# One more seven-product pair in the first half of each four-group feed-forward part

## The chip, the cores and the metric

The kernel runs on one core of one Trainium2 chip. A time is the device time of one execution in microseconds (us). A profiled execution also has a span, from its first to its last instruction.

## What is computed

A two-layer causal decoder trunk on 256 tokens of width 2048, all in float32. Layer 0 mixes by gated spatial products and memory attention, layer 1 by latent attention and memory attention. Each layer ends with the gated feed-forward block that the change touches:

```python
def conv_ffn(h, w_up, cw, cb, w_down):      # h (256, 2048), D_FF = 5632
    a = h @ w_up                            # (256, 11264): gate and value halves
    ap = jnp.pad(a, ((0, 0), (CONV_W - 1, 0), (0, 0)))
    c = sum(ap[:, k:k + S] * cw[k] for k in range(CONV_W)) + cb
    gate, val = c[..., :D_FF], c[..., D_FF:]
    return (jax.nn.silu(gate) * val) @ w_down
...
x = x + conv_ffn(rmsnorm(x, g_ffn[l]), w_ffn_up[l], conv_w[l], conv_b[l], w_ffn_down[l])
```

## The kernel before

**Precision.** A float32 product is made of three TensorE products. An operand is split into a high part (ScalarE, ACT below, copies it to the `fp32r` type) and a low part (VectorE, DVE below, subtracts the high part from the operand), and high x high, high x low and low x high are added in PSUM. Weights come through `raw` (the float32 block that SP's queue loads, 4 buffers, in the down product also `gate`, 2 buffers) and are split to `whi` (4 buffers) and `wlo` (5 buffers).

**Parts.** The 5632 inner columns of the feed-forward block are worked off in parts of 4, 4 and 3 groups of 512 (`FF_GROUPS`). For each part the kernel makes the up product (per group one run of 8 chunks for the gate and one for the value, a chunk being 512 KB of weights and 24 matmuls of 256 columns), then `ev` makes the gated result `h`, and then `down_phase` runs twice: the first half for output columns 0 to 1023, the second half for 1024 to 2047. So there are four four-group parts in the program, two in each layer, in which a half works off 8 pairs of 128-row blocks.

**Pairs.** A plain pair takes 8 block products, 24 matmuls of 512 columns. A seven-product pair (`fast_pair`, a scheme in the manner of Strassen) takes 7, 21 matmuls, but wants sums and differences of its operands. On the side of `h`, `ev` writes quarters of the gated result into the tile `src` (one buffer), makes sums and differences in it, and splits it into a high and a low form of 896 or 1024 columns. On the weight side four sums of half blocks, `t13` and `t24`, are split beside the second row block (`y`) and the left half of the first (`x`). The two parts of this left half go to `one`, which in a four-group part is the same single buffer as `src`. So `one` can only be written after the last read of the `src` before it.

**Where the sums are made.** For three pairs of a first half (`FF_EARLY`) DVE adds them during the part's last up product and they wait in SBUF: two pairs in the tile `sums`, the third in `xs` (2 buffers). For some (`FF_STORED`) they are made during an earlier up product, or during the layer's `w_out` product, and written to DRAM by GpSimd's (POOL's) queue; the half reads them back into `xs` or into `staged` (`FF_STAGED`). A stored case has its loads at chunk n, its four adds at n + 5 and its two stores at n + 8. For the rest (`late_sums`) DVE adds them in the half itself.

**Order.** `FF_FAST` gives for each half the pairs that take seven products, and the order of all of them. Within the engines a list scheduler sets the order of instructions when the program is built; on the chip each engine's queue runs in that order. PSUM has 8 banks: in a half with seven-product pairs four hold the outputs (`e00`, `e01`, `e10`, `e11`) and four hold products that `between` copies to `staged` after the last seven-product pair. `e11` takes plain pairs' products alone. Each output bank is added to the tile `xt` by DVE at the end (`added`).

**The end.** In the last half of layer 1, `Last.evict` makes the squares for the final norm column by column; the last bank comes in two pieces of 256 columns.

Of the kernel before, what the change touches and what calls it, by code (L numbers as in the profile page):

```python
# [8 lines left out]
F32 = mybir.dt.float32  # L9
# [4 lines left out]
ALU = mybir.AluOpType  # L14
AX = mybir.AxisListType

P = 128
D = 2048
# [12 lines left out]
THETA = 10000.0  # L31
EPS = 1e-6
FF_GROUPS = (4, 4, 3)
FF_EARLY = {4: (2, 6, 5), 3: (1, 2, 4)}
FF_STORED = {
# [4 lines left out]
}  # L40
FF_STAGED = {4: (5, 1), 3: (5, 0)}
FF_FAST = {
    4: (((2, 3, 4, 6, 5), (0, 1, 5, 2, 7, 3, 6, 4)), ((2, 3, 4, 6, 5), (0, 2, 1, 3, 5, 4, 7, 6))),
    3: (((1, 2, 4, 5), (0, 3, 1, 2, 4, 5)), ((), (0, 1, 2, 3, 4, 5))),
}

# [35 lines left out]
class Kernel:  # L82
# [119 lines left out]


    def gemm_tm(self, src, nkb, ncol, lhs, evict, nk=2, gain=None, hooks={}, late=0):
        accs = [self.psum() for _ in range(2)]
        nch = nkb // nk
# [56 lines left out]
    def rstd(self, out, sums, n, pool, tag):  # L263
        nc = self.nc
        shape = list(out.shape)
        v = self.tmp(pool, shape, tag + "v", 1)
        r = self.tmp(pool, shape, tag + "r", 1)
        q = self.tmp(pool, shape, tag + "q", 1)
        nc.vector.tensor_scalar(v, sums, 1.0 / n, EPS, ALU.mult, ALU.add)
        nc.scalar.activation(r, v, AF.Sqrt)  # L270
        nc.vector.reciprocal(r, r)
        nc.vector.tensor_tensor(q, r, r, ALU.mult)
        nc.vector.scalar_tensor_tensor(q, q, -0.5, v, ALU.mult, ALU.mult)
        nc.vector.scalar_tensor_tensor(out, q, 1.5, r, ALU.add, ALU.mult)
# [487 lines left out]
    def stored_sums(self, l, case, pool):  # L762
        part, k, ph = case
        dn = self.t["w_ffn_down"][l][sum(FF_GROUPS[:part]) * 512 :]
        order = mybir.DependencyInfo(mybir.DependencyClass.NoSync, mybir.DependencyReason.DATA)
        add = lambda o, a, b: self.tc.keep_in_program_order(self.nc.vector.tensor_tensor(o, a, b, ALU.add))  # L766
        left, right, c = slice(0, 512), slice(512, 1024), 1024 * ph
        held = []

        def load(out, in_):  # L770
            ins = self.nc.sync.dma_start(out=out, in_=in_)
            self.tc.add_manual_dep(ins.ins, self.last_raw, order, reason="behind")

        def loads():
            held.extend(self.tmp(pool(), [P, 1024], "xs", 2) for _ in range(2))
            t13, t24 = held
            x, y = (dn[(2 * k + i) * P : (2 * k + i + 1) * P, c : c + 1024] for i in range(2))
            load(out=t13, in_=x)
            load(out=t24[:, left], in_=y[:, right])
            load(out=t24[:, right], in_=y[:, left])  # L780

        def adds():
            t13, t24 = held
            add(t13[:, left], t13[:, left], t13[:, right])
            add(t13[:, right], t13[:, right], t24[:, left])
            add(t24[:, left], t24[:, left], t13[:, left])
            add(t24[:, right], t24[:, right], t24[:, left])

        def stores():
            kept = self.stored[l, *case] = self.dram.tile([P, 2, 1024], F32, name=self.uid("stored"))  # L790
            for i in range(2):
                self.nc.gpsimd.dma_start(out=kept[:, i], in_=held[i])  # L792

        return loads, adds, stores

    def storing(self, l, part, pool):
        hooks = {}
        for n, case in FF_STORED[part].items():
            loads, adds, stores = self.stored_sums(l, case, pool)
            for m, f in (n, loads), (n + 5, adds), (n + 8, stores):  # L800
                hooks.setdefault(m // 8, {}).setdefault(m % 8, []).append(f)
        return hooks

    def late_sums(self, raws, pool):
# [29 lines left out]
    def down_phase(self, dn, col, order, fast, lhs, rhs, pool, fp, between, evict, finish, late=0, late_gains=None, hooks={}, sums={}, stored={}):  # L834
# [3 lines left out]
        left, right = slice(0, 512), slice(512, 1024)  # L838
# [4 lines left out]
        total = dict(todo)  # L843
# [15 lines left out]
        kept = []  # L859
        last_fast = [k for k in order if k in fast][-1:]  # L860
        for n, k in enumerate(order):
# [8 lines left out]
            load = lambda o, a: self.behind(self.nc.sync.dma_start(out=o, in_=a))  # L870
            row = lambda i, c: load(raws[i][:, :c], dn[(2 * k + i) * P : (2 * k + i + 1) * P, col : col + c])
            blocks = sums.get(k)
            if kept_sums is None:
                row(0, 1024 if blocks is None else 512)
                row(1, 1024)
            else:
                if (k, col // 1024) == FF_STAGED[len(order) // 2]:
                    tile = self.tokens.staged[:, 1].rearrange("p m c -> p (m c)")
                    blocks = [tile[:, i * 1024 : (i + 1) * 1024] for i in range(2)]
                else:  # L880
                    blocks = [self.tmp(pool, [P, 1024], "xs", 2) for _ in range(2)]
                row(1, 1024)
                for i in (1, 0):
                    load(blocks[i], kept_sums[:, i])
                row(0, 512)
# [26 lines left out]
        with self.tc.manual_schedule(engines={ET.PE, ET.DVE, ET.Activation}):  # L912
# [9 lines left out]
            k, ws = kept[-1]  # L922
# [510 lines left out]


class Tokens:
    places = ("hx0", 0), ("hx1", 0), ("hx2", 0), ("hx3", 0)

    def __init__(self, kernel, pool):
        self.k, self.nc, self.pool = kernel, kernel.nc, pool
# [134 lines left out]


class Last(Tokens):
    places = ("kT1", 32), ("mv1", 0), ("hx", 0), ("hx3", 0)

    def __init__(self, kernel, pool):
        super().__init__(kernel, pool)  # L1580
# [19 lines left out]
    def evict(self, tb, half, acc, piece=None, meanwhile=lambda: None):  # L1600
        k, nc, xt, sums = self.k, self.nc, self.xt, self.sums
        c0, n = (0, 512) if piece is None else (256 * piece, 256)
        j, o = self.added(tb, half, acc, c0, n)
        c = slice(j * 512 + c0, j * 512 + c0 + n)
        if not self.last:
            return
        one = lambda x: x[:, tb : tb + 1]
        part, r, q, v, gb = self.part, self.r, self.q, self.v, self.gb
        junk = k.tmp(self.pool, [P, 512], "fjunk", 2)
        if piece == 1:  # L1610
            nc.vector.tensor_tensor_reduce(
                out=junk[:, :n], in0=o, in1=o, scale=-0.5 / D, scalar=one(part), op0=ALU.mult, op1=ALU.add, accum_out=one(v)
            )
        else:
            nc.scalar.activation(junk[:, :n], o, AF.Square, accum_out=sums[:, tb, j : j + 1])
        if piece == 0:
            self.added(tb, half, acc, 256, 256)
        meanwhile()
        if j < 3 and not (tb and j == 2):
            nc.vector.tensor_tensor(o, o, gb[:, c], ALU.mult)  # L1620
# [4 lines left out]
            if tb:  # L1625
                nc.vector.tensor_tensor(o, o, gb[:, c], ALU.mult)
        if j == 3:
            if piece != 1:
                total = one(part) if piece == 0 else one(v)
                nc.vector.tensor_scalar(total, sums[:, tb, 3:4], -0.5 / D, one(part), ALU.mult, ALU.add)  # L1630
            if piece == 0:
                return
            nc.scalar.activation(one(r), one(v), AF.Sqrt, scale=-2.0)
            nc.vector.reciprocal(one(r), one(r))
            nc.vector.scalar_tensor_tensor(one(q), one(r), one(r), one(v), ALU.mult, ALU.mult)
            nc.vector.scalar_tensor_tensor(one(r), one(q), 1.5, one(r), ALU.add, ALU.mult)
# [36 lines left out]
```

## Time and profile before

| | |
|---|---|
| median of 3 runs | 2021.81 us (2021.78 to 2022.23) |
| profiled execution, its own time | 2022.45 us |
| its span | 2020.7 us |
| TensorE (PE) busy | 2010.5 us, 99% of the span |
| DVE busy | 1665.6 us, 82% |
| ACT busy | 1184.9 us, 59% |
| POOL busy | 129.1 us, 6% |
| moved by DMA | 463.27 MB, 229 GB/s over the span |

PE, PEld (its weight loads), DVE, ACT, POOL and SP are the engines of the profile; SP only issues transfers. A line such as L719 is a line of the kernel, and often a helper's: all splits of weights in the down product have L718 (ACT) and L719 (DVE). Matmuls are pipelined, so the duration of one is longer than the distance from its start to the start of the next. In a view in order of time a row gives start, duration, engine, line, operation, output and inputs.

### The profile page before, as it was taken

Reading aid. Unit: us, or ns where it says so; the run is one execution under the profiler, and the core shown is the slowest. Engines: PE = TensorE matmul, PEld = TensorE weight load, DVE = VectorE, ACT = ScalarE, POOL = GpSimd, SP = SyncE. Lnnn points to the kernel's source line nnn. Section 1 sums busy time; section 2 is a strip of 40 time slices with the busy share of each in tenths; the row PEclk is TensorE's granted clock in tenths of the full one; section 3 lists DMA queues with packets and bytes.
Section 4 is the critical chain, followed back from the end, with each engine's and each line's share of the span. In section 5 each row is a group of like instructions: output and inputs, shape, how many; then the busy total and the mean of one; then the engine's idle time right before and its main releaser. Section 6 shows DMA issues by size and latency. Waiting matters only on the chain.

```text
span 2020.7 us, 38415 instructions
## 1 busy us (share of the span) xinstructions
PE 2010.5 (99%) x15098; PEld 1905.3 (94%) x15098; DVE 1665.6 (82%) x2519; ACT 1184.9 (59%) x1687; POOL 129.1 (6%) x205
## 2 busy tenths in 40 slices
PE   9999999999999999999999999999999999999998
PEld 8989999999989999899989999999988999889996
DVE  6866767788898788988988787778889878898897
ACT  6754744555665556655576675455566555665565
POOL 0000013100000000000002142400000000000000
PEclk9999999999999999999999999999999999999999
DMA  8775567888668786678566636788867878667865
GB/s 256 232 217 180 166 217 254 232 293 276 210 235 266 246 275 211 233 234 261 185 224 187 183 113 203 235 242 288 275 206 237 273 237 275 206 235 233 275 187 179
DMA packets 269897, 463.27 MB, mean 229 GB/s; under 512 B 77774, under 2 KB 85268, under 8 KB 269716
## 3 DMA queue, kind: packets, MB, share of 16 engines
q1 hardware_dynamic: 264340, 441.40, 68.6%
q0 software_dynamic: 5184, 18.88, 2.6%
q8 instruction: 118, 1.93, 0.4%
q14 instruction: 63, 0.52, 0.1%
q10 hardware_dynamic: 192, 0.54, 0.1%
HBM read 435.06 MB, written 20.97 MB: 226 GB/s over the span
## 4 chain that ended last, share of the span: by engine, by line
PE 98%; DVE 1%; ACT 1%; DMA 0%; issue 0%; SPq 0%; ACTq 0%; DVEq 0%
PE ps L166 22%; PE ps L167 22%; PE ps L169 22%; PE ps L850 7%; PE ps L851 7%; PE ps L852 7%; PE ps L198 2%; PE ps L199 2%; PE ps L200 2%; PE ps L533 1%; DMA raw<-in_w_ffn_down 0%; PE ps L613 0%; PE ps L612 0%; PE ps L611 0%; PE ps L415 0%; PE ps L1324 0%
## 5 line engine op out<-in xcount | busy, mean ns | idle before, releaser
L127 ACT ACTIVATE whi<-raw 128x1024 fp32r<-128x1024 f32 x484 | 513.7, 1062 | 528.7 <-PE ps L167 387.3
L128 DVE TENSOR_TENSOR wlo<-raw,whi 128x1024 fp32r<-128x1024 f32 x484 | 597.1, 1238 | 204.2 <-ACT whi L127 200.6
L166 PE MATMUL ps<-xhl,whi 128*128 128x256 f32 x3264 | 763.3, 277 | 0.0
L167 PE MATMUL ps<-xhl,whi 128*128 128x256 f32 x3264 | 761.6, 276 | 0.0
L167 PEld LDWEIGHTS ps<-xhl,whi 128*128 128x128 f32 x3264 | 612.8, 188 | 0.4
L166 PEld LDWEIGHTS ps<-xhl,whi 128*128 128x128 f32 x3264 | 612.8, 188 | 0.4
L169 PE MATMUL ps<-xhl,wlo 128*128 128x256 f32 x3264 | 438.0, 276 | 0.0
L169 PEld LDWEIGHTS ps<-xhl,wlo 128*128 128x128 f32 x3264 | 401.1, 188 | 0.0
L851 PE MATMUL ps<-wlo,h 128*128 128x512 f32 x354 | 137.1, 388 | 0.1
L719 DVE TENSOR_TENSOR wlo<-raw,whi 128x1024 fp32r<-128x1024 f32 x94 | 113.9, 1219 | 20.9 <-ACT whi L718 20.0
L718 ACT ACTIVATE whi<-raw 128x1024 fp32r<-128x1024 f32 x94 | 98.4, 1054 | 52.7 <-PE ps L167 32.2
L166 PE MATMUL ps<-mainhl,whi 128*128 128x256 f32 x512 | 119.7, 277 | 0.0
L167 PE MATMUL ps<-mainhl,whi 128*128 128x256 f32 x512 | 119.3, 276 | 0.0
L852 PE MATMUL ps<-whi,h 128*128 128x512 f32 (+1 forms) x306 | 118.4, 388 | 0.0
L967 ACT ACTIVATE c<-a,cT 128x256 f32<-128x256 f32 x176 | 99.0, 591 | 29.4 <-DVE a L246 28.4
L850 PE MATMUL ps<-whi,h 128*128 128x512 f32 x354 | 108.3, 389 | 0.0
L167 PEld LDWEIGHTS ps<-mainhl,whi 128*128 128x128 f32 x512 | 96.0, 188 | 0.0
L166 PEld LDWEIGHTS ps<-mainhl,whi 128*128 128x128 f32 x512 | 95.9, 188 | 0.0
L792 POOL DMA_DIRECT2D stored<-xs x36 | 19.8, 550 | 1158.9 <-DVE xs L766 985.1
L718 ACT ACTIVATE whi<-xs 128x1024 fp32r<-128x1024 f32 x60 | 62.7, 1058 | 47.6 <-DVE xs L808 23.7
L133 DVE SCALAR_TENSOR_TENSOR wlo<-raw,gT,whi 128x512 fp32r<-128x512 f32 x96 | 71.0, 779 | 21.3 <-ACT whi L132 21.2
L852 PE MATMUL ps<-whi,hhx 128*128 128x512 f32 x216 | 84.0, 389 | 0.0
(401 smaller groups left out, 3131.6 us busy)
## 6 DMA issues: line engine op xcount, KB each, us to landing
raw<-in_w_ffn_up SPq DMA_DIRECT2D x352, 512.0 KB, 4.6
raw<-in_w_ffn_down SPq DMA_DIRECT2D x102, 512.0 KB, 5.8
raw<-in_w_out SPq DMA_DIRECT2D x64, 512.0 KB, 4.4
raw<-in_w_in_a SPq DMA_DIRECT2D x56, 512.0 KB, 4.4
gate<-in_w_ffn_down SPq DMA_DIRECT2D x38, 512.0 KB, 5.0
stored<-xs POOLq DMA_DIRECT2D x36, 512.0 KB, 5.3
raw<-in_w_mem_kv SPq DMA_DIRECT2D x31, 512.0 KB, 3.6
xs<-in_w_ffn_down SPq DMA_DIRECT2D x24, 512.0 KB, 6.5
```

Source lines behind the costliest of these rows:

```text
L127: nc.scalar.activation(hi[:, :n], raw[:, :n], AF.Copy)
L128: nc.vector.tensor_tensor(lo[:, :n], raw[:, :n], hi[:, :n].bitcast(F32), ALU.subtract)
L133: nc.vector.scalar_tensor_tensor(lo[:, s], raw[:, s], gains[k], hi[:, s].bitcast(F32), ALU.mult, ALU.subtract)
L166: mm(acc[:, :S], wh, x[:, :S], start=first, stop=False)
L167: mm(acc[:, :S], wh, x[:, S:], start=False, stop=False)
L169: mm(acc[:, :S], wl, x[:, :S], start=False, stop=last)
L718: self.behind(self.nc.scalar.activation(hi, w, AF.Copy))
L719: self.behind(self.nc.vector.tensor_tensor(lo, w, hi.bitcast(F32), ALU.subtract))
L850: mm(o, xh, wh, start=start, stop=False)
L851: mm(o, xh, wl, start=False, stop=False)
L852: mm(o, xl, wh, start=False, stop=stop)
L967: nc.scalar.activation(c, a, AF.Identity, scale=w(2), bias=w(3))
```

## The change

In the first half of the four-group parts pair 7 becomes a seven-product pair, so 6 of 8 are. The order becomes: the plain pairs 0 and 1 first, then 2, 5, 4, 3, 6, 7. The early pairs are 2, 5 and 4 instead of 2, 6 and 5. The pairs 3, 6 and 7 read stored sums, 3 and 7 into the two halves of `staged`, 6 into `xs`; before, only pair 3 did, and pair 4 had late sums. The second halves stay as they were. So 12 cases a layer are stored for the four-group parts instead of 8, spaced by 8 chunks instead of 11 to 14, and a case's loads and stores are put into the program one by one (n, n + 1, n + 5, n + 6, n + 7). The forms of `h` for pair 7 take 2 x 1024 columns, so a fifth tile `hx4` (`hx2` in layer 1) is used; to make room for it, two temporaries of `rstd` take the ring `sq`. In `Last.evict` the term of the first piece is added after DVE has taken in the second piece.

```diff
-FF_EARLY = {4: (2, 6, 5), 3: (1, 2, 4)}
+FF_EARLY = {4: (2, 5, 4), 3: (1, 2, 4)}
...
-    1: {8: (1, 2, 1), 22: (1, 5, 1), 36: (1, 4, 1)},
+    1: {2: (1, 6, 0), 10: (1, 7, 0), 18: (1, 2, 1), 26: (1, 5, 1), 34: (1, 4, 1)},
...
-FF_STAGED = {4: (5, 1), 3: (5, 0)}
+FF_STAGED = {4: {(3, 0): 1, (7, 0): 0, (5, 1): 1}, 3: {(5, 0): 1}}
...
-    4: (((2, 3, 4, 6, 5), (0, 1, 5, 2, 7, 3, 6, 4)), ((2, 3, 4, 6, 5), (0, 2, 1, 3, 5, 4, 7, 6))),
+    4: (((2, 3, 4, 6, 5, 7), (0, 1, 2, 5, 4, 3, 6, 7)), ((2, 3, 4, 6, 5), (0, 2, 1, 3, 5, 4, 7, 6))),
...
-        v = self.tmp(pool, shape, tag + "v", 1)
+        v, q = (self.tmp(pool, shape, *(("sq", 2) if tag == "rb" else (tag + x, 1))) for x in "vq")
         r = self.tmp(pool, shape, tag + "r", 1)
-        q = self.tmp(pool, shape, tag + "q", 1)
...
-            loads, adds, stores = self.stored_sums(l, case, pool)
-            for m, f in (n, loads), (n + 5, adds), (n + 8, stores):
-                hooks.setdefault(m // 8, {}).setdefault(m % 8, []).append(f)
+            for m, f in zip((0, 1, 5, 6, 7), self.stored_sums(l, case, pool)):
+                hooks.setdefault((n + m) // 8, {}).setdefault((n + m) % 8, []).append(f)
...
-                if (k, col // 1024) == FF_STAGED[len(order) // 2]:
-                    tile = self.tokens.staged[:, 1].rearrange("p m c -> p (m c)")
+                home = FF_STAGED[len(order) // 2].get((k, col // 1024))
+                if home is not None:
+                    tile = self.tokens.staged[:, home].rearrange("p m c -> p (m c)")
...
-    places = ("hx0", 0), ("hx1", 0), ("hx2", 0), ("hx3", 0)
+    places = ("hx0", 0), ("hx1", 0), ("hx2", 0), ("hx3", 0), ("hx4", 0)
...
         if piece == 1:
+            nc.vector.tensor_scalar(one(part), sums[:, tb, 3:4], -0.5 / D, one(part), ALU.mult, ALU.add)
             nc.vector.tensor_tensor_reduce(
...
         if piece == 0:
             self.added(tb, half, acc, 256, 256)
+            return
...
-            if piece != 1:
-                total = one(part) if piece == 0 else one(v)
-                nc.vector.tensor_scalar(total, sums[:, tb, 3:4], -0.5 / D, one(part), ALU.mult, ALU.add)
-            if piece == 0:
-                return
+            if piece is None:
+                nc.vector.tensor_scalar(one(v), sums[:, tb, 3:4], -0.5 / D, one(part), ALU.mult, ALU.add)
```

Three places show how the instructions move; all four four-group parts have them in the same order, and the first is shown. DVE, at the start of the first half, before. `src_6516` is the quarter tile of pair 6, the pair whose `h` is made last in seven-product form; `wlo_6634`, `wlo_6638` and `wlo_6642` are the low parts of `y`, `t24` and `t13` of pair 5, the half's first seven-product pair; `src_6645` is the low part of its left half of `x`; `hhx_584` is the plain `h` of pair 7:

```order
L719 TENSOR_TENSOR wlo_6634<-raw_6630,whi_6633 128x1024
L989 TENSOR_TENSOR gate_5969<-gate_5969,c_6532 128x256
L989 TENSOR_TENSOR gate_5969<-gate_5969,c_6541 128x256
L719 TENSOR_TENSOR wlo_6638<-xs_6292,whi_6637 128x1024
L1008 TENSOR_TENSOR h_4226<-src_6516,h_4226 128x896
L255 TENSOR_TENSOR hhx_584_4230<-gate_5969,hhx_584_4230 128x256 x2
L719 TENSOR_TENSOR wlo_6642<-xs_6291,whi_6641 128x1024
L719 TENSOR_TENSOR src_6645<-raw_6629,src_6645 128x512
```

The same place of the changed kernel. `src_6542` is pair 6's quarter tile and `src_6562` pair 7's, `ps_6580` is the bank `e11`, and `src_6673` is the left half of `x` of pair 2, now the first seven-product pair:

```order
L718 TENSOR_TENSOR wlo_6662<-raw_6658,whi_6661 128x1024
L718 TENSOR_TENSOR wlo_6666<-sums_6030,whi_6665 128x1024
L1008 TENSOR_TENSOR h_4239<-src_6542,h_4239 128x896
L996 TENSOR_TENSOR src_6562<-gate_5995,c_6558 128x2x128
L1000 TENSOR_TENSOR src_6562<-gate_5995,c_6566 128x256
L1503 TENSOR_TENSOR xt<-ps_6580,xt 128x512
L718 TENSOR_TENSOR wlo_6670<-sums_6030,whi_6669 128x1024
L1002 TENSOR_TENSOR src_6562<-src_6562 128x256
L1003 TENSOR_TENSOR src_6562<-src_6562 128x128
L1004 TENSOR_TENSOR src_6562<-src_6562 128x128
L1008 TENSOR_TENSOR hhx_587_4242<-src_6562,hhx_586_4241 128x1024
L718 TENSOR_TENSOR src_6673<-raw_6657,src_6673 128x512
```

Between pair 6's low part and the first `x` stand now seven rows of pair 7's quarters and the bank `e11`, beside `t13`. ACT has its own side of it in the changed kernel: the high part of pair 7's `h` (out of `src_6562`), then the high part of `x` into the same buffer, then `y` and `t24` of the next pair, pair 5:

```order
L1007 ACTIVATE h_4239<-src_6542 128x896
L717 ACTIVATE whi_6669<-sums_6030 128x1024
L1007 ACTIVATE hhx_586_4241<-src_6562 128x1024
L717 ACTIVATE src_6673<-raw_6657 128x512
L717 ACTIVATE whi_6701<-raw_6698 128x1024
L717 ACTIVATE whi_6705<-sums_6030 128x1024
```

Behind the copy of `x` stand the splits that pair 5 needs first. PE, the last rows of pair 2 and the first of pair 5 in the changed kernel (`whi_6669` is the high part of `t13`, `ps_6581` the bank of the product with `x`):

```order
L849 MATMUL ps_6582<-whi_6669,h_4239 128x512
L849 MATMUL ps_6584<-whi_6669,h_4239 128x512
L850 MATMUL ps_6582<-wlo_6670,h_4239 128x512
L851 MATMUL ps_6582<-whi_6669,h_4239 128x512
L850 MATMUL ps_6584<-wlo_6670,h_4239 128x512
L851 MATMUL ps_6584<-whi_6669,h_4239 128x512
L849 MATMUL ps_6581<-src_6673,h_4239 128x512
L850 MATMUL ps_6581<-src_6673,h_4239 128x512
L851 MATMUL ps_6581<-src_6673,h_4239 128x512
L849 MATMUL ps_6577<-whi_6701,h_4239 128x512
```

The three products with `x` are the 19th to 21st of the pair; the second of them reads the low part. Before, counted from the start of the first seven-product pair, they were the 15th, 22nd and 23rd, with first matmuls of the next pair between them. The transfers of the half's second part on SP's queue, changed kernel, from the loads of pair 4 (`gate`) to those of pair 7:

```order
L869 DMA gate_6737<-in_w_ffn_down 128x512
L869 DMA gate_6738<-in_w_ffn_down 128x1024
L869 DMA raw_6778<-in_w_ffn_down 128x1024
L869 DMA staged_6576<-stored_5057 128x1024 x2
L869 DMA raw_6777<-in_w_ffn_down 128x512
L869 DMA raw_6820<-in_w_ffn_down 128x1024
L869 DMA xs_6822<-stored_5341 128x1024
L869 DMA xs_6821<-stored_5341 128x1024
L869 DMA raw_6819<-in_w_ffn_down 128x512
L869 DMA gate_6864<-in_w_ffn_down 128x1024
L869 DMA staged_6576<-stored_5638 128x1024 x2
L869 DMA gate_6863<-in_w_ffn_down 128x512
```

Three pairs in a row read 512 KB + 1 MB + 256 KB each; `staged` takes the memory of the early tile `sums` of pairs 2 and 5, and `xs` that of pair 4.

More of the change, by code (lines that the diff above doesn't have):

```diff
@@ L772, in load, with loads @@
             self.tc.add_manual_dep(ins.ins, self.last_raw, order, reason="behind")
[L774 to L780, printed above, removed]
+        def loads(i):
+            held.append(self.tmp(pool(), [P, 1024], "xs", 2))
+            w = dn[(2 * k + i) * P : (2 * k + i + 1) * P, c : c + 1024]
+            if i == 0:
+                load(out=held[0], in_=w)
+            else:
+                load(out=held[1][:, left], in_=w[:, right])
+                load(out=held[1][:, right], in_=w[:, left])
         def adds():
@@ L787, in adds, with stores @@
             add(t24[:, right], t24[:, right], t24[:, left])
[L789 to L794, printed above, removed]
+        def stores(i):
+            if i == 0:
+                self.stored[l, *case] = self.dram.tile([P, 2, 1024], F32, name=self.uid("stored"))
+            self.nc.gpsimd.dma_start(out=self.stored[l, *case][:, i], in_=held[i])
+        return [lambda: loads(0), lambda: loads(1), adds, lambda: stores(0), lambda: stores(1)]
     def storing(self, l, part, pool):
@@ L1576 @@
 class Last(Tokens):
-    places = ("kT1", 32), ("mv1", 0), ("hx", 0), ("hx3", 0)
+    places = ("kT1", 32), ("mv1", 0), ("hx", 0), ("hx2", 0), ("hx3", 0)
     def __init__(self, kernel, pool):
```

4 rows, old and new, of the table FF_STORED are left out of this document.

## The prediction

> **What bounds the kernel now.** I read the page first (parts 1 and 5), then the list of who waited for whom, then a table of stretches, then the first four-group part in order of time.
>
> ```profile
> span 2020.7 us, 38415 instructions
> PE 2010.5 (99%) x15098; PEld 1905.3 (94%) x15098; DVE 1665.6 (82%) x2519; ACT 1184.9 (59%) x1687; POOL 129.1 (6%) x205
> ...
> L851 PE MATMUL ps<-wlo,h 128*128 128x512 f32 x354 | 137.1, 388 | 0.1
> ```
>
> The profiled execution took 2022.45 us, 1.75 over its span and 0.64 over the median of 2021.81. TensorE is busy nearly throughout, and the list of its waits is short:
>
> ```profile
> PE ps L500 <- DVE ones L297: 1.1, 1, 1.1
> PE ps L850 <- ACT staged L1482: 0.2, 1, 0.2
> PE ps L613 <- DVE pT L255: 0.2, 1, 0.2
> ```
>
> So a matmul that goes is a gain, and any wait of PE is a full loss: no slack later takes it up. Up product, first half, second half of the first four-group part, and two stretches of the next up product (us, busy time by engine, clock, DMA share, GB/s):
>
> ```profile
> core 0: us, PE busy (x) PEld busy (x) DVE busy (x) ACT busy (x) POOL busy (x), PEclk, DMA share, GB/s
> 354.00:528.00 174.00, 174.00 (x1536) 173.95 (x1535) 146.10 (x221) 95.77 (x123) 9.60 (x14) 1.00 0.83 259
> 528.10:568.30 40.20, 40.20 (x179) 32.99 (x178) 36.51 (x52) 26.97 (x34) 0.00 (x0) 1.00 0.56 190
> 568.30:608.50 40.20, 40.20 (x179) 33.15 (x178) 36.87 (x40) 26.69 (x31) 0.00 (x0) 1.00 0.78 268
> ...
> 608.70:630.45 21.75, 21.75 (x193) 21.73 (x192) 21.17 (x24) 10.73 (x13) 0.00 (x0) 1.00 0.84 281
> ...
> 717.45:739.20 21.75, 21.75 (x195) 21.75 (x194) 15.26 (x24) 11.99 (x17) 0.53 (x1) 1.00 0.97 331
> ```
>
> In the halves DVE is busy 91% of the time, so it cannot run far ahead.
>
> **The matmuls removed.** 3 per first half, 12 in all; the program has 12 fewer. Their price is not the mean of 388 ns, which overlaps the next matmul, but the distance of starts:
>
> ```profile
> 528.11 0.40 PE L850 MATMUL ps<-whi,hhx 128*128 128x512 f32 x1
> ...
> 538.78 0.39 PE L852 MATMUL ps<-whi,hhx 128*128 128x512 f32 x1
> 539.01 0.39 PE L850 MATMUL ps<-whi,h 128*128 128x512 f32 x1
> ...
> 542.18 0.39 PE L850 MATMUL ps<-src,h 128*128 128x512 f32 x1
> ...
> 568.28 0.39 PE L850 MATMUL ps<-whi,hhx 128*128 128x512 f32 x1
> ```
>
> The first row opens the first half, the last the second: 40.17 us for 3 x 24 + 5 x 21 = 177 matmuls, 0.227 each. So 12 x 0.227 = 2.72 us are saved. The Trainium skill (TensorE: Matmul & The Clock Gate, "Wait — 56ns, not 53.3ns?") gives 215.7 ns from start to start at 512 columns and a warm clock; with it the term would be 2.59. The trace's 227 decides.
>
> **The new wait.** The third and fourth rows above are the last matmul of plain pair 1 and the first of the first seven-product pair, the fifth its first product with the left half of `x`. What feeds it (first rows DVE, last two ACT):
>
> ```profile
> 534.92 1.22 DVE L719 TENSOR_TENSOR wlo<-raw,whi 128x1024 fp32r<-128x1024 f32 x1
> ...
> 536.73 1.21 DVE L719 TENSOR_TENSOR wlo<-xs,whi 128x1024 fp32r<-128x1024 f32 x1
> 537.86 1.08 DVE L1008 TENSOR_TENSOR h<-src,h 128x896 fp32r<-128x896 f32 x1
> ...
> 539.62 1.23 DVE L719 TENSOR_TENSOR wlo<-xs,whi 128x1024 fp32r<-128x1024 f32 x1
> 540.77 0.69 DVE L719 TENSOR_TENSOR src<-raw,src 128x512 fp32r<-128x512 f32 x1
> ```
>
> ```profile
> 538.53 1.06 ACT L718 ACTIVATE whi<-xs 128x1024 fp32r<-128x1024 f32 x1 [1.27 <-PE ps L852]
> 539.50 0.62 ACT L718 ACTIVATE src<-raw 128x512 fp32r<-128x512 f32 x1
> ```
>
> Now `x` is copied into `src` at 539.50, after pair 6's low part has left it (538.94), and is ready at 540.12, 2 us before its matmul at 542.18. In the changed program pair 7's quarters go through the same buffer in between. Their durations, and that of an output bank's addition:
>
> ```profile
> L1002 DVE TENSOR_TENSOR src<-src x28: 407/416/420, 448.2 to 1961.2; 128x256 f32<-128x256 f32 x28
> L1003 DVE TENSOR_TENSOR src<-src x28: 272/283/292, 449.3 to 1963.2; 128x128 f32<-128x128 f32 x28
> ...
> L1007 ACT ACTIVATE h<-src x28: 934/940/1046, 452.2 to 1966.3; 128x896 fp32r<-128x896 f32 x20, 128x1024 fp32r<-128x1024 f32 x8
> L1008 DVE TENSOR_TENSOR h<-src,h x24: 1079/1084/1219, 453.5 to 1967.7; 128x896 fp32r<-128x896 f32 x16, 128x1024 fp32r<-128x1024 f32 x8
> ```
>
> ```profile
> 554.97 0.68 DVE L1503 TENSOR_TENSOR xt<-ps,xt 128x512 f32<-128x512 f32 x1
> ```
>
> DVE, in the new order and in the old one's time: `y` at 534.92 as before, `t24` 1.13 later (the distance between the rows 536.73 and 537.86), pair 6's low part 537.18 to 538.26, two quarter rows of 0.42 to 539.0. Then `e11`, which waits for pair 1's last matmul (538.78 + 0.39 = 539.17): to 539.9. `t13` to 541.0. Three quarter rows, each reading what the one ahead wrote, 0.42 + 0.28 + 0.28: to 542.0. ACT's high part of 1024 columns, 1.05: to 543.07. DVE's low part, 1.22: to 544.33. Only now is the buffer free: ACT copies `x` (0.62) to 544.98, DVE subtracts (0.69) to 545.70.
>
> PE wants the high part at 539.01 + 18 x 0.227 = 543.09 and gets it at 545.02: 1.93. The low part, one matmul later, at 545.74 instead of 545.25: 0.49. Behind the copy of `x` ACT has the splits of the next pair: `y` is there in time, `t24` at 546.91 and not 546.65 (ACT's splits come 0.97 apart, as 538.53 and 539.50 do): 0.3. Together 2.7 us in a part, and the order is the same in all four: +10.9. If the three quarter rows overlap and `e11` costs nothing it is 1.8 (total 7.2); if each handover on the chain costs 0.1 more, 3.6 (14.4). I take 2.7, by the rows of the same operations.
>
> **Smaller terms.** With pair 4's late sums a small stall goes:
>
> ```profile
> 562.93 2.01 ACT L718 ACTIVATE whi<-xs 128x1024 fp32r<-128x1024 f32 x2 [2.42 <-DVE xs L808]
> ...
> 563.49 1.29 PE L850 MATMUL ps<-whi,h 128*128 128x512 f32 x4
> ```
>
> Four such matmuls take 3 x 0.227 + 0.39 = 1.07, so it is 0.2 in a part, 0.85 in four (bounds 0 and 1.2). At the end DVE no longer stands before the last piece:
>
> ```profile
> 2013.12 0.21 DVE L1630 TENSOR_SCALAR fpart<-fsums,fpart 128x1 f32<-128x1 f32 x1 [0.30 <-ACT fjunk L1615]
> 2013.25 0.41 DVE L1503 TENSOR_TENSOR xt<-ps,xt 128x256 f32<-128x256 f32 x1
> 2013.69 0.48 DVE L1611 CUSTOM_DVE_ANT_0 fjunk<-xt,fpart 128x256 f32<-128x256 f32 x1
> ```
>
> The piece can be added from about 2012.75 on, the small row follows at 2013.15, and the last one comes at 2013.42: -0.25 (bounds -0.4 and +0.1).
>
> The four more stored cases a layer cost DVE four adds of 0.68 each, ACT nothing, and SP's queue waits for a store before the next case's loads. I cost them at nothing, because the splits of the up product run ahead until the buffers are full:
>
> ```profile
> ACT whi L127 <- PE ps L167: 387.3, 283, 3.3
> ACT whi L127 <- DMA raw<-in_w_ffn_up: 62.8, 40, 6.4
> ```
>
> A wait of 6.4 us for a load passes without a row of PE. If the cover goes: one stretch, 608.70, has DVE at 21.17 of 21.75; with 2.7 more it overruns by 2.1, twice in the program, 4.2 at most. The changed temporaries of `rstd`, the fifth tile and `w_out`'s third case add no instruction that PE waits for (0 to 0.5).
>
> Sum: -2.72 + 10.9 - 0.85 - 0.25 = +7.1. Own time 2022.45 + 7.1 = 2029.5; against the median 2028.9.
>
> **Rivals.**
> *The chain is covered* (0.11). The scheduler may rightly count on `x` in time, and handovers may overlap more than I assume. Break-even is a stall of (2.72 + 0.85 + 0.25) / 4 = 0.95 us a part, so `x` would have to come 1.8 us earlier. Against it: each step waits for the one ahead through one buffer, and the chain's ACT and DVE rows are measured. Without any stall: 2021.81 - 3.8 = 2018.0, not slower.
> *The stored pieces come late too* (0.13). `staged` is free when pair 5's `t13` is split (about 549.4). From then the queue holds 5.0 MB up to pair 7's last row. At 268 / 0.78 = 344 GB/s that is 14.4 us plus a landing of some 2, pair 7's `t13` at 565.2, wanted at 566.2: 1 us to spare. With the medians below it fails:
>
> ```profile
> xs<-stored SPq DMA_DIRECT2D x24, 512.0 KB, 6.5
> ```
>
> 549.5 + 6.5 = 556.0 against 555.4 for pair 3's `t24`, and the same again behind it: up to 1.5 a part, 2028.9 + 6 = 2034.9. For it also speaks that ACT has waited for such a load without PE's suffering, but with the lead that the new stall uses up:
>
> ```profile
>   DMA xs<-stored: 3.2, 2
> ```
>
> *The up product loses its lead* (0.07): +2 to +4.2, 2031 to 2033.
> *The clock drops behind the stall* (0.03). A gate that halves the clock for one pair, 21 x 0.227 = 4.8 us more a part, would give 2048. Against it, the granted clock after PE's last matmul at 2012.3:
>
> ```profile
> 2016.00:2020.00 4.00, 0.00 (x0) 0.00 (x0) 0.31 (x1) 0.50 (x1) 0.00 (x0) 0.66 0.68 262
> ```
>
> A mean of 0.66 between 1 and one half puts the drop near 2017.3, 5 us after the work ended; the stall is half as long. The Trainium skill (the same page, "Part 1: The HAM clock gate") puts the idle window at about 3.4 us; by that rule too 2.7 us would mostly pass.
>
> **How the numbers follow.** My forecast, 2028.9, has 0.66; its own range, with 1.8 to 3.6 a part, is 2025 to 2032.5. To hold 8 in 10 I go from 2024 to 2035, which takes in the late pieces and the up product, and leaves out the covered chain and the clock. A measurement of this kernel tells about 0.2%, 4 us, from no change. The covered chain ends just inside it (0.07) or just below (0.04), and the low end of my forecast inside (0.07): faster 0.04, same 0.14, slower 0.82.
>
> **What would show it.** In the profile after: PE's waits list matmuls of L849 and L850 waiting for ACT and DVE `src`, some 2 us, four times, 15 us after the start of each four-group first half; ACT's copy of the first `x` begins near 544.4 instead of 539.5; the span from 528.1 to the second half's first matmul is about 42, not 40.2; 351 instead of 354 matmuls in a part. It is wrong if `x` is there by 543.1, if PE goes on with other matmuls, or if waits for `staged` and `xs` loads outweigh `src`.

## The result, and the profile after

The changed kernel takes 2037.74 us, the median of six executions of which five lie between 2036.55 and 2040.04 (their own median is 2037.32) and one, of 5174.58 us, stands apart from all others; the kernel before takes 2022.09 us beside it. The ratio is 1.0077, 95% interval 1.0064 to 1.009: some 15.6 us slower. The direction was forecast, the size was not (2028.9, with a range up to 2035).

The profile is that of a repeat of the changed kernel, one execution of 2038.54 us. The head of its page, which answers to that of before:

```profile
span 2036.8 us, 38594 instructions
...
PE 2015.5 (99%) x15086; PEld 1905.5 (94%) x15086; DVE 1681.5 (83%) x2551; ACT 1191.5 (58%) x1691; POOL 133.5 (7%) x221
```

PE has 12 matmuls fewer and is busy 5 us longer: some of them run slower. PE's list of waits (us in total, times, longest):

```profile
PE ps L849 <- ACT src L717: 8.9, 5, 2.8
PE ps L499 <- DVE ones L296: 1.1, 1, 1.1
PE ps L849 <- ACT staged L1482: 0.7, 1, 0.7
PE ps L850 <- DVE src L718: 0.7, 3, 0.2
PE ps L850 <- DVE wlo L718: 0.5, 1, 0.5
PE ps L849 <- ACT whi L717: 0.4, 2, 0.2
```

The forecast wait for `src` is there. Of its five times four are the first seven-product pair, once in each four-group part. The fifth is a later pair in the second part, for which no `src` chain was forecast. But the list holds some 11 us of new waits, and the kernel lost 15.6.

So I measured the four parts, each from the start of its first matmul to the start of its last. Before, each took 80.39 us. They begin now at 528.22, 788.88, 1492.83 and 1749.40 and take 86.34, 84.55, 82.25 and 83.79: 15.4 us more in all, which is nearly the whole loss (the last three-group part has 0.5 more). Four parts with the same instructions in the same order differ by 4 us. The third is the plainest. PE there, in order of time (start, duration, engine, line, operation, output and input):

```profile
1507.59 0.39 PE L851 MATMUL ps<-whi,h 128*128 128x512 f32 x1
1509.81 0.50 PE L849 MATMUL ps<-src,h 128*128 128x512 f32 x1 [1.84 <-ACT src L717]
1510.54 0.51 PE L850 MATMUL ps<-src,h 128*128 128x512 f32 x1 [0.23 <-DVE src L718]
1510.88 0.39 PE L851 MATMUL ps<-src,h 128*128 128x512 f32 x1
1511.11 1.34 PE L849 MATMUL ps<-whi,h 128*128 128x512 f32 x4
```

From 1507.59 to 1511.11 four matmuls should take 0.91 and take 3.52: 2.6, and 0.3 more follows in the next pair. The fourth part has the same first rows, and then something else:

```profile
1769.30 0.63 PE L850 MATMUL ps<-wlo,h 128*128 128x512 f32 x1
1769.73 0.63 PE L851 MATMUL ps<-whi,hkT 128*128 128x512 f32 x1
1770.16 0.63 PE L850 MATMUL ps<-wlo,h 128*128 128x512 f32 x1
1770.58 0.63 PE L851 MATMUL ps<-whi,hkT 128*128 128x512 f32 x1
```

These wait for nothing, so no list of waits has them, but they start 0.43 us apart and not 0.227. The table of stretches says why. Its rows are, in pairs, the stall and what follows it, from the first part to the fourth (us, busy time by engine, granted clock, DMA share, GB/s):

```profile
core 0: us, PE busy (x) PEld busy (x) DVE busy (x) ACT busy (x) POOL busy (x), PEclk, DMA share, GB/s
543.00:548.00 5.00, 2.00 (x6) 1.03 (x6) 3.00 (x6) 2.53 (x3) 0.00 (x0) 0.81 0.57 188
549.00:553.00 4.00, 4.00 (x11) 3.12 (x10) 4.00 (x5) 2.86 (x5) 0.00 (x0) 0.51 0.04 10
803.00:807.00 4.00, 1.94 (x8) 1.08 (x7) 2.12 (x3) 2.71 (x4) 0.00 (x0) 1.00 0.33 132
807.00:811.00 4.00, 4.00 (x18) 3.01 (x17) 4.00 (x5) 4.00 (x5) 0.00 (x0) 1.00 0.02 4
1507.00:1511.00 4.00, 1.94 (x8) 1.07 (x7) 2.18 (x3) 2.71 (x4) 0.00 (x0) 1.00 0.31 126
1511.00:1515.00 4.00, 4.00 (x18) 2.99 (x17) 4.00 (x5) 4.00 (x6) 0.00 (x0) 1.00 0.00 0
1763.50:1767.50 4.00, 1.94 (x8) 1.07 (x7) 2.11 (x3) 2.71 (x4) 0.00 (x0) 1.00 0.36 145
1768.00:1772.00 4.00, 4.00 (x12) 2.96 (x11) 4.00 (x5) 3.39 (x5) 0.00 (x0) 0.57 0.05 12
```

In the first and the fourth part the granted clock falls to a half with the stall, and PE, though busy throughout, gets through 11 or 12 matmuls in 4 us in place of 18. The second part keeps its clock and loses 2.3 us elsewhere, in its pairs 3 and 6. ACT there:

```profile
815.65 1.06 ACT L717 ACTIVATE whi<-staged 128x1024 fp32r<-128x1024 f32 x1 [1.21 <-DMA staged<-stored]
817.81 1.06 ACT L717 ACTIVATE whi<-staged 128x1024 fp32r<-128x1024 f32 x1 [1.10 <-DMA staged<-stored]
820.56 0.63 ACT L717 ACTIVATE src<-raw 128x512 fp32r<-128x512 f32 x1 [1.68 <-DMA raw<-in_w_ffn_down]
```

These splits wait for loads, and PE's fifth wait for `src`, at 821.24, is the last of them passed on. So three things stand beside the chain: the clock, late loads, and a first part whose stall is larger than that of the others.

### The profile page after: what moved, and what is told of

Read it like the earlier page. It is cut to its first block, busy times and chain, and to the rows that moved or that the text cites. A ratio compares the mean times of both kernels' runs of the same rounds, so it can differ in the third digit from the quotient of the medians.

```text
span 5172.9 us, 38594 instructions
## 1 busy us (share of the span) xinstructions
PE 5163.8 (100%) x15086; PEld 4547.6 (88%) x15086; DVE 1721.7 (33%) x2551; ACT 1213.8 (23%) x1691; POOL 126.2 (2%) x221
## 4 chain that ended last, share of the span: by engine, by line
PE 100%; DVE 0%; ACT 0%; issue 0%; ACTq 0%
PE ps L169 22%; PE ps L167 22%; PE ps L166 22%; PE ps L850 7%; PE ps L849 7%; PE ps L851 7%; PE ps L200 2%; PE ps L199 2%; PE ps L198 2%; PE ps L532 1%; PE ps L1324 0%; PE ps L612 0%; PE ps L611 0%; PE ps L610 0%; PE ps L414 0%; PE ps L1110 0%
## 5 line engine op out<-in xcount | busy, mean ns | idle before, releaser
L166 PE MATMUL ps<-xhl,whi 128*128 128x256 f32 x3264 | 1689.1, 523 | 0.0
L167 PE MATMUL ps<-xhl,whi 128*128 128x256 f32 x3264 | 1685.0, 522 | 0.0
L167 PEld LDWEIGHTS ps<-xhl,whi 128*128 128x128 f32 x3264 | 1413.4, 433 | 3.9 <-issue 3.7
L166 PEld LDWEIGHTS ps<-xhl,whi 128*128 128x128 f32 x3264 | 1412.6, 433 | 3.1 <-issue 2.5
L169 PE MATMUL ps<-xhl,wlo 128*128 128x256 f32 x3264 | 1049.7, 521 | 0.0
L169 PEld LDWEIGHTS ps<-xhl,wlo 128*128 128x128 f32 x3264 | 1012.4, 433 | 0.0
L850 PE MATMUL ps<-wlo,h 128*128 128x512 f32 x354 | 282.8, 800 | 0.0
L166 PE MATMUL ps<-mainhl,whi 128*128 128x256 f32 x512 | 268.8, 531 | 0.0
L167 PE MATMUL ps<-mainhl,whi 128*128 128x256 f32 x512 | 268.1, 530 | 0.0
L849 PE MATMUL ps<-whi,h 128*128 128x512 f32 x354 | 240.6, 796 | 0.0
L167 PEld LDWEIGHTS ps<-mainhl,whi 128*128 128x128 f32 x512 | 225.3, 441 | 0.2 <-issue 0.2
L166 PEld LDWEIGHTS ps<-mainhl,whi 128*128 128x128 f32 x512 | 225.0, 440 | 0.5 <-issue 0.4
L849 PEld LDWEIGHTS ps<-whi,h 128*128 128x128 f32 x354 | 122.7, 347 | 78.7 <-issue 77.3
L169 PE MATMUL ps<-mainhl,wlo 128*128 128x256 f32 x512 | 167.5, 529 | 0.0
L851 PEld LDWEIGHTS ps<-whi,h 128*128 128x128 f32 x306 | 103.3, 337 | 72.5 <-issue 71.9
```

What stands on the lines that cost most here:

```text
L166: mm(acc[:, :S], wh, x[:, :S], start=first, stop=False)
L167: mm(acc[:, :S], wh, x[:, S:], start=False, stop=False)
L169: mm(acc[:, :S], wl, x[:, :S], start=False, stop=last)
L849: mm(o, xh, wh, start=start, stop=False)
L850: mm(o, xh, wl, start=False, stop=False)
L851: mm(o, xl, wh, start=False, stop=stop)
```

## The experiments

**The changed kernel once more.** No edit; its profile is the one above.

> The changed kernel once more, for its profile: it took 15.6 us more than the kernel before, 8.5 more than forecast. Theory A (the chain of pair 7's quarters through the buffer src): four waits of PE's products with x in the first halves, and they are 4 to 6 us each instead of 2.7, or 2.7 with a granted clock near one half for about 5 us behind each (the mean clock of its runs, 0.9965 against 0.999, would be 5 us over the whole span). Theory B (stored sums come late): matmuls of pairs 3, 6 and 7 wait for parts of staged and xs, 8 us in all. Theory C (stored cases 8 chunks apart): rows of PE in the up products wait for raw loads, 8 us in all, and the first halves are only some 2 us longer.

2037.83 us. Theory A's plain form, 2.9 us a part, holds in the third part; its form with the half clock in two others. B's late loads are there too, in one part. C's rows of PE in the up products are absent. So the theories are not exclusive, and each was then taken away by itself.

**The spacing of the stored cases by itself.** The kernel before with the new `FF_STORED` and the pieces put in one by one; the sums of pairs 6 and 7 are stored and not read.

> The kernel before with the changed kernel's table of stored cases and its finer pieces alone: 12 instead of 8 cases a layer for the four-group parts, 8 chunks apart; the halves are as before and leave the new sums of pairs 6 and 7 unread. Theories A and B: no change, 2021.5 to 2023. Theory C: 2026 to 2030, with PE waiting for raw in the up products or in the w_out products.

2022.33 us, ratio 1.0002 (0.9993 to 1.0012): no cost in the kernel before. Its first part still begins with less lead: the last low part of the up product ends 2.9 us before its matmul, against 6.2 in the kernel before. That part takes 80.38 us all the same, as long as in the kernel before.

**Pair 7 plain again.**

```diff
-    4: (((2, 3, 4, 6, 5, 7), (0, 1, 2, 5, 4, 3, 6, 7)), ...
+    4: (((2, 3, 4, 6, 5), (0, 1, 2, 5, 4, 3, 6, 7)), ...
-FF_STAGED = {4: {(3, 0): 1, (7, 0): 0, (5, 1): 1}, ...
+FF_STAGED = {4: {(3, 0): 1, (5, 1): 1}, ...
     (and the stored cases (0, 7, 0) and (1, 7, 0) taken out)
```

> The changed kernel with pair 7 plain again (5 seven-product pairs, 354 matmuls a part, no stored sums for pair 7; the order of pairs, the early pairs, the stored sums of pair 6, the spacing of the cases, the end as in the changed kernel). Theory A: no quarters in front of x, 2021 us, within 0.2% of the kernel before. Theory B: pairs 3 and 6 still read stored sums one behind the other, some 2025. Theory C: 10 instead of 8 cases for the four-group parts of a layer and still 8 chunks apart, 2025 to 2029.

2020.61 us, ratio 0.9993 (0.9983 to 1.0002). All four parts take 80.04 us without a stall. The new order, the stored sums of pair 6 and the end are free or better; all that is lost hangs on pair 7. Against 80.39 this is 0.35 a part; 0.22 of it stood at the matmuls that waited for pair 4's late sums, the rest in smaller delays that the new order doesn't have.

**The left half of `x` of the first pair elsewhere.**

```diff
+            if n == 2 and not col and len(order) == 8:
+                room = self.tmp(fp, [P, 1024], "gate", 2, F32R)
...
-        one = self.one or self.tmp(self.tokens.pool, [P, 1024], "src", 1, F32R)
+        one = room or self.one or self.tmp(self.tokens.pool, [P, 1024], "src", 1, F32R)
```

(Pair 4, whose rows load into `gate`, then takes the two buffers in the other order.)

> The changed kernel with the left half of x of the first seven-product pair of each four-group first half in a free buffer of the ring gate instead of src, so that it doesn't wait for pair 7's quarters. Theory A: all of the extra time goes, 2018 us (2021.8 less 3.8 for 12 matmuls, the late sums and the end), no wait on src in PE's list. Theory B: the forecast's 2.7 a part go and the late pieces stay, 2026 to 2027. Theory C: the same, 2026 to 2027, with waits in the up products.

2032.18 us, ratio 1.0048 (1.0031 to 1.0065). None of the forecasts: the wait did not go, it moved on by one pair. The quarters still stand in `src`, and the next pair's `x` waits for them:

```profile
PE ps L849 <- ACT src L717: 3.3, 4, 1.0
```

**The quarters elsewhere.** The other side of the conflict: pair 7's quarters go into the free buffer of `gate`.

```diff
-                            quarters["src"] = tokens.quarters()
+                            quarters["src"] = self.tmp(fp, [P, 1024], "gate", 2) if n == 14 and ng == 4 else tokens.quarters()
```

> The changed kernel with pair 7's quarters in the free buffer of the ring gate instead of src; x of the first seven-product pair can go into src right behind pair 6's low part again. Theory A (src chain, with what the clock and the loads do behind its stall): the stall of 2.9 us in each part goes, and with it the stretches of half clock (0.50 to 0.52 behind two of the four stalls, some 4 us) and most of the late loads of part 2; 2018 us, 351 matmuls a part without a wait, about 79.7 us a part. Theory B (stored pieces late whatever the chain does): stalls of some 2 us a part in pairs 3, 6 and 7, as in the second part of the changed kernel (waits for staged and raw at 815 to 824 us); without the chain they come earlier and grow, 2022 to 2028. Theory D (the first part enters with 2 us less lead of the splits): a stall of some 0.7 us at the first seven-product pair of the first part stays, 2019.

2042.46 us, ratio 1.0105 (1.0088 to 1.0122): slower still. PE waits for `src` no more. But `gate` is also where pair 4's rows are loaded, and the quarters hold that buffer until their low part is made (DVE, 805.32 plus 1.23 in the second part), so the load is issued only at 806.58 and has landed 4 us later, when ACT has long been waiting. ACT in the second part:

```profile
804.89 0.63 ACT L717 ACTIVATE src<-raw 128x512 fp32r<-128x512 f32 x1 [0.65 <-PE ps L851]
810.48 1.06 ACT L717 ACTIVATE whi<-gate 128x1024 fp32r<-128x1024 f32 x1 [4.96 <-DMA gate<-in_w_ffn_down]
```

PE stalls for 3.1 to 3.3 us in each part, and the clock halves behind all four.

**The quarters in gate, the loads out of their way.** Besides the edit above:

```diff
-                if n % 3 == (2 if col else 1) and n > 1:
+                if n == 5 if not col and len(order) == 8 else n % 3 == (2 if col else 1) and n > 1:
```

> Pair 7's quarters in the free buffer of gate once more, but the first half's loads go into gate for pair 3 (the sixth) alone, and not for pairs 4 and 7, so that no load of pair 4 waits for the quarters. Quarters in gate with pair 4's loads there had cost 2042.5: in place of x, the splits of pair 4 waited, 3.1 to 3.3 us, for a buffer that the quarters held until 547, with half clock behind it in all four parts. Theory A (buffers shared with pair 7's quarters, and the clock behind the stall): no stall of over 0.5 us is left in three or four of the parts, the granted clock is 0.999, 2018 us (at most 2020 with the late loads of one part). Theory B (the stored pieces are late whatever the quarters do): 1.5 to 2 us a part in pairs 3, 6 and 7 are left, with some half clock, 2024 to 2030.

2020.56 us, ratio 0.9993 (0.9984 to 1.0002). The second part, ACT: `x` is copied right behind `t13`, and pair 7's high part 3 us behind it, out of the way.

```profile
794.26 1.06 ACT L717 ACTIVATE whi<-sums 128x1024 fp32r<-128x1024 f32 x1 [2.41 <-PE ps L851]
795.23 0.61 ACT L717 ACTIVATE src<-raw 128x512 fp32r<-128x512 f32 x1
...
798.94 1.06 ACT L1007 ACTIVATE hhx<-gate 128x1024 fp32r<-128x1024 f32 x1 [0.18 <-DVE gate L1004]
```

Three parts take 79.36 us without a stall, and in them no load is late and no clock is halved. So the half clock came with the stall. The late loads went with it too, but for them the stall is not separated from the other buffers that this edit gives to the loads of pairs 4 and 7. The first part takes 81.13, with 1.6 us of stall: there something else is left.

**A longer stall.** The changed kernel with four rows more on the chain:

```diff
+        for _ in range(more):        # 4 for the first seven-product pair of a four-group first half, else 0
+            self.behind(self.nc.vector.tensor_tensor(b11[0], x[:, left], x[:, left], ALU.add))
```

> The changed kernel with four more rows of DVE (512 columns, some 0.6 us apart) ahead of x of the first seven-product pair: the stall grows by 2.4 us a part, from 2.9 to 5.3. If a stall costs only itself: 2037.8 + 4 x 2.4 = 2047.4, the mean granted clock stays near 0.996. If the clock halves behind a stall that takes most of a window of activity: all four parts, not two of them, now show a granted clock of 0.5 for 3 to 4 us, that is some 1.7 us more in each of the two that were spared, 2050 to 2052, mean clock 0.993 to 0.994.

2049.19 us, ratio 1.0135 (1.012 to 1.015), the mean clock 0.994. The gap ahead of `x` is 4.95 us in each part (from start to start, less the usual 0.227). Behind it, in all four:

```profile
549.00:552.00 3.00, 3.00 (x10) 2.29 (x10) 3.00 (x3) 3.00 (x4) 0.00 (x0) 0.60 0.00 0
809.00:812.00 3.00, 3.00 (x8) 2.32 (x8) 2.75 (x4) 3.00 (x5) 0.00 (x0) 0.50 0.00 0
1516.00:1519.00 3.00, 3.00 (x8) 2.35 (x9) 2.98 (x3) 3.00 (x4) 0.00 (x0) 0.50 0.00 0
1777.30:1780.30 3.00, 3.00 (x8) 2.36 (x8) 2.75 (x4) 3.00 (x5) 0.00 (x0) 0.52 0.02 5
```

The rows decide for the clock: a half in all four parts. The time by itself would not: the median is 11.4 us up, the profiled execution 10.6, of which 10.2 lie in the four parts. There 10.9 are the longer gaps (2.95 in three parts, 2.0 in the first, and not 2.4 each); the half clock costs 1.0 to 2.1 a part, 6.3 in all where the changed kernel had 3.9; and against that the second part's late loads (2.3) and the first part's wait at `t13` (0.8) do not show here.

**The stored cases of the first part.** What does the first part have that the others lack? Its up product waited most for loads. ACT's waits from 400 to 528 us, before and changed:

```profile
ACT whi L127 <- DMA raw<-in_w_ffn_up: 15.7, 12, 3.1
```

```profile
ACT whi L127 <- DMA raw<-in_w_ffn_up: 33.9, 17, 4.6
```

PE did not wait there, but the last low part of the up product ends 1.6 us before its matmul instead of 6.2, and the first half begins with that. So one run takes the changed kernel with another table alone, and one the version above with it:

```diff
-    0: {16: (0, 3, 0), 24: (0, 6, 0), 32: (0, 7, 0), 40: (1, 3, 0)},
-    1: {2: (1, 6, 0), 10: (1, 7, 0), 18: (1, 2, 1), 26: (1, 5, 1), 34: (1, 4, 1)},
+    0: {20: (0, 3, 0), 32: (0, 6, 0), 44: (0, 7, 0)},
+    1: {2: (1, 6, 0), 10: (1, 7, 0), 18: (1, 2, 1), 26: (1, 5, 1), 34: (1, 4, 1), 42: (1, 3, 0)},
```

> The changed kernel with that table of stored cases alone (20, 32, 44 in the first part, the case of pair 3 for the second part at 42 of the second). If the first part's larger stall (0.8 us at t13 and 2.95 instead of 2.0 at x) is the lost lead, it becomes like the others, 2.9 us in all, and the time falls by some 1.7, and by up to 2 more where the clock no longer halves behind it: 2034 to 2036.5. If the spacing has no part in it, 2037.8.

2035.13 us, ratio 1.0062 (1.0049 to 1.0076), 2.7 us less. The waits for up loads from 400 to 528 us are gone, and the lead at the end is 7.4 us. `y` of the first part's first seven-product pair has its low part 2.2 us earlier on DVE, changed kernel and this one:

```profile
537.26 1.23 DVE L718 TENSOR_TENSOR wlo<-raw,whi 128x1024 fp32r<-128x1024 f32 x1
```

```profile
535.10 1.22 DVE L718 TENSOR_TENSOR wlo<-raw,whi 128x1024 fp32r<-128x1024 f32 x1
```

The gap at `x` in the first part is now 2.0 us, like that of the changed kernel's third part, and the wait at `t13` is gone. The clock halved at three of the four stalls here, in the first three parts, where the changed kernel had it in the first and the fourth.

The table alone does not fix the lead, though. The six profiled kernels with a case in every 8 chunks of the first part ended its up product with 1.6 to 6.2 us of lead. The 6.2 is the longer stall's, whose up product is the changed kernel's, and there the wait at `t13` is absent too. Both kernels with the cases 12 chunks apart had 7.4.

> quarters_gate_later with the stored cases of the first part 12 chunks apart (20, 32, 44) and the case of pair 3 for the second part moved from chunk 40 of the first part to chunk 42 of the second. quarters_gate_later took 2020.6: three parts of 79.36 us without a stall, the first 81.13 with 1.6 us of stall, because it starts with 2.1 us of lead of the low-part splits instead of 6.2. If the spacing keeps the lead from recovering, the lead is back at 5 to 6 us at 525, the first part takes 79.4, and the time is 2018.9 (2018.5 to 2019.5). If the fifth tile or rstd's changed temporaries cost the lead, it stays at 2 us and the time at 2020.5.

2019.82 us (2018.62 to 2024.72), ratio 0.9991 (0.9982 to 1.0), the lowest median of all. The four parts, whole:

```profile
core 0: us, PE busy (x) PEld busy (x) DVE busy (x) ACT busy (x) POOL busy (x), PEclk, DMA share, GB/s
528.50:607.80 79.30, 79.30 (x352) 65.67 (x351) 73.75 (x91) 55.45 (x65) 0.00 (x0) 1.00 0.74 258
782.20:861.50 79.30, 79.30 (x352) 65.67 (x351) 73.80 (x91) 55.49 (x65) 0.00 (x0) 1.00 0.72 252
1481.00:1560.00 79.00, 79.00 (x351) 65.44 (x350) 73.44 (x91) 55.05 (x65) 0.00 (x0) 1.00 0.73 258
1734.70:1814.00 79.30, 79.30 (x350) 65.30 (x350) 74.41 (x93) 56.32 (x65) 0.00 (x0) 1.00 0.74 259
```

PE is busy throughout at full clock; three parts take 79.36 us and the fourth, which begins with 3.2 us of lead, 79.64. The median is 0.9 us above the forecast and outside its range. Part of that is the fourth part; another may be a wait in the last three-group part, which the other kernels have at 0 to 1.5:

```profile
PE ps L849 <- ACT staged L1482: 1.0, 1, 1.0
```

With the interval ending at 1.0, it is not shown to beat the kernel before; it does beat the changed kernel by 18 us.

## Why the prediction was right and wrong

The parts without a stall (79.36 us) give the account of the 15.4 us:

| term | forecast | measured |
|---|---|---|
| 12 matmuls fewer | -2.72 | -2.7: 80.04 - 79.36 = 0.68 a part |
| pair 4's late sums, measured with the new order | -0.85 | -1.4: 80.39 - 80.04 = 0.35 a part |
| the chain through `src` | +10.9 | +11.6: 82.25 - 79.36 = 2.89 in the third part, four times |
| stored cases in the up product | 0 (a rival, 0.07) | +1.7 in the first part: 86.34 - 79.36 - 2.89 - 2.4 |
| half clock behind the stall | 0 (a rival, 0.03) | +3.9: 1.5 in the fourth part (83.79 - 82.25), 2.4 in the first |
| late stored pieces | 0 (a rival, 0.13) | +2.3 in the second part (84.55 - 82.25) |

(The 2.4 are about twelve distances of 0.43 in place of 0.227; what the first part then has over the third is put down to its lead. The line between these two is an estimate. The gaps bear it out: the first part's gap at `x` is 0.95 longer than the third's, and its wait at `t13` takes 0.8.) The last three rows, 7.9 us, are nearly the whole of what the forecast of 7.1 us missed: the sum had all three at nothing.

**The chain was right**, and row by row. ACT's copy of `x` was to begin 16.25 us after the first matmul (544.36 on the time scale of before); in the third part it begins at 1509.13, 16.30 after. The gap at the low part was put at 0.49 and is 0.50. These are the third part's rows of pair 7's high part, its low part and the copy of `x`, which were to begin 13.9, 15.0 and 16.25 us after the first matmul and begin 13.95, 15.04 and 16.30 after it:

```profile
1506.78 1.06 ACT L1007 ACTIVATE hmv<-src 128x1024 fp32r<-128x1024 f32 x1 [2.46 <-DVE src L1004]
1507.87 1.22 DVE L1008 TENSOR_TENSOR hhx<-src,hmv 128x1024 fp32r<-128x1024 f32 x1 [1.12 <-ACT hmv L1007]
1509.13 0.63 ACT L717 ACTIVATE src<-raw 128x512 fp32r<-128x512 f32 x1 [1.29 <-DVE hhx L1008]
```

The first half's length was put at 42 us; in the third part it is 42.4. Taking away the buffer's second use, and with it the loads into the buffer that the quarters moved to, took away the stall; nothing that computes was changed.

**The matmuls and the end were right.** DVE's step from the last matmul to the last column sum took 1.48 us in place of 1.67: -0.19, forecast -0.25.

**The step that failed first: the clock.** I argued that it fell 5 us after PE's last matmul, and that the stall was half as long. That is one observation of a delay and not a threshold. Over the kernels that have one stall in each four-group part (by the gap ahead of the matmul that waits):

| gap | half clock behind it |
|---|---|
| 0.9 to 1.1 us (`x` elsewhere) | 1 of 4 |
| 2.0 to 2.4 us (the changed kernel, cases moved) | 4 of 7 |
| 2.95 to 3.3 us (the changed kernel's first part, quarters in gate) | 5 of 5 |
| 4.95 us (longer stall) | 4 of 4 |

Where it fell it cost about 1.0 to 2.4 us, and not the 4.8 that the rival charged for a whole pair. Why equal stalls had either outcome stands in the clock records of the traces, which give each stretch of half clock with its start and length. All their edges ahead of PE's last matmul lie whole multiples of 3.413 us apart within an execution, and a stretch lasts 3.413 or 6.827 us. So there is a grid of windows, and what counts is where the gap falls on it. The third part's gap is cut by an edge near its middle. The fourth's, of the same 2.0 us, lies almost whole in one window, and the next window runs at half clock (changed kernel, two windows of the third part, two of the fourth):

```profile
core 0: us, PE busy (x) PEld busy (x) DVE busy (x) ACT busy (x) POOL busy (x), PEclk, DMA share, GB/s
1505.28:1508.69 3.41, 2.69 (x12) 1.88 (x11) 2.22 (x5) 1.06 (x1) 0.00 (x0) 1.00 0.83 276
1508.69:1512.10 3.41, 2.06 (x7) 1.21 (x8) 2.46 (x4) 2.97 (x4) 0.00 (x0) 1.00 0.00 0
1764.69:1768.10 3.41, 1.49 (x5) 0.86 (x5) 2.46 (x3) 2.40 (x3) 0.00 (x0) 1.00 0.07 26
1768.10:1771.51 3.41, 3.41 (x9) 2.55 (x9) 3.41 (x5) 2.80 (x5) 0.00 (x0) 0.50 0.02 5
```

Count as idle what a distance of starts ahead of which PE waited has over 0.227 us. Then, in the ten traces that have clock records (the kernel before, the repeat and the eight variants), between 500 and 2000 us, each of the 14 windows at full clock with 1.86 us of idle or more is followed by half clock, and no window with 1.77 or less. That line, near half a window, is read from these rows; no run was made to test it. It also fits the 5 us that I had argued from: in the kernel before, the window in which PE stopped had 1.7 us of idle, the next was empty, and only at its end did the clock fall.

The changed kernel's runs spread over 3.5 us and those of the kernel before, beside them, over 0.5. That the place of the drops makes the difference is not shown: the last version, which has no such stall, spread over 6.1.

The Trainium skill (TensorE: Matmul & The Clock Gate, "Part 1: The HAM clock gate") says that the window of activity is free-running; the trace agrees, by the grid. It puts the drop behind at least one idle window of about 3.4 us; there the measurement differs, for 1.86 us of idle in one window was enough. My reading of that rule, that 2.7 us would mostly pass, was wrong. The same page's 426.7 ns from start to start at 512 columns and a half clock agrees with the 0.43 here.

**The second: rivals taken for alternatives.** I gave the late pieces 0.13 and the clock 0.03, as cases beside mine. Both hang on my own forecast. The clock falls with the stall. And the stall delays the split of pair 5's `t13`, and with it the moment at which `staged` is free. In the second part its load is issued at 810.32, 21.4 us after the first matmul; in the version without the stall at 799.58, 17.4 after, and no load is late. I had counted 1 us to spare with the stall in place. That was too thin for one part in four. Why the second part alone lost by it is open: its first loads are issued at the same moment after the first matmul as those of the third and the fourth, but in the 5 us from there 207 GB/s were moved, and 253 and 247 in the other two.

**The third: the cover for the stored cases.** The costed loss of the lead was 2.1 us at one place, and PE indeed waited nowhere in the up product. But I took a lead that is spent for one that comes back. With a case in every 8 chunks the first part's lead stayed mostly under 5 us and ended at 1.6, and the low part of the first seven-product pair's `y` came 2.2 us late. Moving the cases alone took this away. In the kernel before the same spacing cost nothing, and in the longer stall's execution the lead was 6.2 with it; so the spacing puts the lead at risk, and what it comes to in one execution varies.

The sum of what was shown, -2.7 - 1.4 + 11.6 + 1.7 + 3.9 + 2.3, is the 15.4 us of the four parts.

## What to carry to other kernels

A stall on a busy TensorE is paid more than once: by its length; by half clock behind it, which came in these runs at 4 of 7 gaps of 2.0 to 2.4 us, depending on where they fell on the grid of windows, and at all 9 of 2.95 us or more; and by everything that the delayed engine had to set free. So price a stall with its consequences, and not with consequences as rivals. When a wait comes from a buffer with two uses, ask of each place that one of the uses could move to who else lives there: `x` in another buffer moved the wait by a pair, the quarters in `gate` made it larger, and only with the loads out of `gate` as well was it gone.

## What the hardware showed that I had not expected

The half clock has no row among the waits: PE shows as busy, with matmuls 0.43 us apart. It is seen in the granted clock of a stretch of a few microseconds, or in the distance of starts; the mean over the span, 0.996 in place of 0.999, hides it. And it lasted 3.41 us and 6.83 us at stalls of one length (the longer stall's fourth part and its second), one window and two, so that its price depends on the grid too.
